# Banded attention by whole and half key tiles in a streaming encoder layer: shared transposes and array halves

## The chip, the core and the metric

The kernel runs on one core of a Trainium2 chip. The metric is the device time of one launch in microseconds (us), the median of several runs. Engines are named as in the profile: PE is TensorE (PEld its weight loads), DVE is VectorE, ACT is ScalarE, POOL is GpSimd, SP is SyncE, which issues all DMAs here. PSUM is where TensorE writes; a bank holds 128 x 512 fp32 numbers.

## The reference

One layer over 2048 new frames (the prompt) and 8 running streams of 16 frames each (the sample), d_model 1024. Cut to what matters here:

```python
# attention: 8 query heads, 2 kv heads of 64; chunk c (64 frames) reads chunks c-2, c-1, c
s = jnp.einsum('bcqgrd,bckgd->bcgrqk', qc, kb) * (SWA_HD ** -0.5)
s = jnp.where(valid, s, NEG_INF)                 # the first chunks have fewer keys
p = sink_softmax(s, sinks)                       # one learned sink per head in the denominator
o = jnp.einsum('bcgrqk,bckgd->bcqgrd', p, vb)
# sample: each stream reads 128 cached keys and its own 16
# retention: 4 heads of 128; one chunk, s is the state of a stream
o = (q k^T * decay) v + (q s) * q_decay
s_new = gamma ** t * s + (k * k_decay)^T v       # the sample has a state for each of 8 streams
# then GroupNorm and gate, output projection, LayerNorm, squared-ReLU MLP (4096), LayerNorm
```

All is fp32.

## The kernel before

The 2176 rows are 17 tiles of 128 (tile 16 is the sample), worked in three groups of 5, 6 and 6 tiles. Each group goes through the stages kv, sq, ret, out and mlp, and a tile's name in the profile carries the group and the stage in which it was made (`sw_1ret`: PSUM tile of kind sw, group 1, stage ret). The big products split each operand into a high and a low part and run as three products of the faster fp32r type (`mm3`); the attention's and retention's own products are plain fp32, and so are the transposes, which are products with the identity.

The order of the program is made when it is built. A planner (`Sched`) keeps an estimated clock for each engine. Each piece of work is a generator that yields the time at which it wants to go on; whenever bulk work is emitted, the planner first lets those generators run whose time has come. Every call (`matmul`, `vtt`, `act`, `dma`) carries a cost, by which the planner's clocks move. So a changed cost, or a changed piece, shifts the order of everything after it on each engine's queue. On the chip each queue runs in order and waits on semaphores.

Tiles come from pools with a fixed number of buffers: `u3` (8, SBUF), `w` (10, weights), `raw` (4), and in PSUM `mm` 2, `rt` 2, `sw` 4 banks.

`swa_task` does the attention of the prompt tiles, one after another, beside the projections. For each of a tile's two chunks it makes scores of 192 keys for 4 heads in 2 pairs (`ps`), row maxima, exponentials with sums (`act`), division by the sum (`vts`), and transposes of the probabilities, padded with zeros to two key tiles of 128; then the product with the values (`pv`). Score products use 64 rows of the array, one kv head in the upper and one in the lower half; value products use 64 columns, one kv head in the left and one in the right half. `swa_sample_task` does the same for the sample, two streams at a time. `ret_task` does retention of one head of one tile; for the sample it works in two halves of 4 streams: it loads the old states (`sold`), masks queries (`qp`) and values (`vm`) by stream, adds four products to `op`, makes four new states in one product of 512 columns (`kvs`), and stores them (`sn`).

Beside this, `first_operands`, `right_operands` and `left_operand` prepare and load split combinations of the MLP's weights, for a scheme that forms seven products in place of eight (a pair of them is counted by `made_d`; `EARLY` is 8). `right_operands` works in group 1's stages in `raw` buffers, and from the MLP on in `w` buffers.

Of the kernel before, what the change touches and what calls it, by code (L numbers as in the profile page):

```python
# [9 lines left out]
F32R = mybir.dt.float32r  # L10
# [163 lines left out]
def tile_layer(ctx: ExitStack, tc: tile.TileContext, A: dict, O: dict):  # L174
# [176 lines left out]
    smask = cst[:, C_SM:C_SM + 8]  # L351
# [162 lines left out]
    def first_operands():  # L514

        for j in range(2):
# [9 lines left out]
            for o, t, args in todo:  # L526
# [8 lines left out]
                yield S.ready(out, eng="ACT")  # L535
# [13 lines left out]
    def right_operands():  # L549
# [8 lines left out]
        def put(j, o, src):  # L558
# [4 lines left out]
            held[0] -= tag == "w"  # L563
            acopy(w[:, 0:512], src)
# [280 lines left out]
    def swa_task(tiles, slot, sq_tasks, qTs, kTall, vall, mixs):  # L845
        gsl = [slice(0, 64), slice(64, 128)]
        for ti, t in enumerate(tiles):
# [6 lines left out]
            w0 = 0 if t > 0 else 1  # L854
            for c in range(2):
                lo = 0 if t > 0 else 128
                lo, hi = (max(lo, 64), 256) if c else (lo, 192)
                yield S.soon(qT, kTall[:, k0:k0 + 2 * P])
                while not (room("sw", 2) and room("u3", 2)):
                    yield S.now + 0.3  # L860
                ps = [take("sw", [P, 2, hi - lo]) for g in range(2)]
                pb = [take("u3", [P, 2, 256]) for g in range(2)]
# [6 lines left out]
                mx, nm, den, es, rec = tiny(4), tiny(4), tiny(4), tiny(4), tiny(4)  # L869
                for g in range(2):  # L870
                    vmax(mx[:, 2 * g:2 * g + 2], ps[g])
                    if c == 0:
                        gzero(pb[g][:, :, 192:256])
                    elif t > 0:
                        gzero(pb[g][:, :, 0:64])
                vstt(nm, mx, -1.0, nsink[:, 0:4], ALU.mult, ALU.min)
                vtt(es, nm, sink[:, 0:4], ALU.add)
                yield S.ready(nm, eng="ACT")
                for g in range(2):
                    for hp in range(2):  # L880
                        i = 2 * g + hp
                        act(pb[g][:, hp, lo:hi], ps[g][:, hp, :], AF.Exp, bias=nm[:, i:i + 1], accum=den[:, i:i + 1])
                drop(*ps)
                act(es, es, AF.Exp)
                yield S.ready(den, es, eng="DVE")
                vtt(den, den, es, ALU.add)
                vrecip(rec, den)
                for g in range(2):
                    for hp in range(2):
                        i = 2 * g + hp  # L890
                        vts(pb[g][:, hp, lo:hi], pb[g][:, hp, lo:hi], rec[:, i:i + 1], None, ALU.mult)
                yield S.soon(*pb)
                pts = []
                for g in range(2):
                    while not (room("sw", 1) and room("u3", 1)):
                        yield S.now + 0.3
                    pt = take("sw", [P, 2, 2, P])
                    for w in range(w0, 2):
                        for hp in range(2):
                            transpose(pt[:, w, hp, :], pb[g][:, hp, 128 * w:128 * w + 128])  # L900
                    drop(pb[g])
                    pts.append(take("u3", [P, 2, 2 * P]))
                    copy(pts[g][:, w0:2, :], pt[:, w0:2].rearrange("p w h r -> p w (h r)"))
                    drop(pt)
                yield S.soon(*pts)
                yield from wait_room("sw")
                pv = take("sw", [P, 256])
                for w in range(w0, 2):
                    for g, gs in enumerate(gsl):
                        matmul(pv[gs, :], vall[:, slot[t] - 1 + w, gs], pts[g][:, w, :], w == w0, w == 1)  # L910
                drop(*pts)
                copy(mixs[ti][:, :, 64 * c:64 * c + 64], pv.rearrange("p (j t) -> p j t", j=4))
                drop(pv)


    def swa_sample_task(ti, si, sq_tasks, qTs, kTall, vall, mix):
# [3 lines left out]
        for hb in range(2):  # L920
# [12 lines left out]
            for pr in range(2):  # L933
# [38 lines left out]
                ov = take("sw", [P, 2, P])  # L972
                for i in range(2):
                    n = 2 * pr + i
                    matmul(ov[:, i, :], cv[:, n, :], pts[:, i, :], True, False)
                    matmul(ov[:, i, :], vn[0:32, n, :], pts[0:32, 2 + i, :], False, True)
                drop(pts)
                for g in range(2):
                    gs = slice(64 * g, 64 * g + 64)
                    for i in range(2):  # L980
                        b = 4 * hb + 2 * pr + i
                        copy(mix[gs, :, 16 * b:16 * b + 16], ov[gs, i, 64 * g:64 * g + 64].rearrange("p (j t) -> p j t", j=4))
# [5 lines left out]
    def ret_task(t, h, ps, rope_t, mix):  # L988
# [32 lines left out]
        if smp:  # L1021
            matmul(op, sm, v, True, False)
            for hb in range(2):
                yield from wait_room("u3", 4)
                sold, qp, vm, sn = [take("u3", sh) for sh in ([P, 4, P], [P, 640], [P, 4, P], [P, 4, P])]
                dma(sold, A["st"][h][:, 4 * hb:4 * hb + 4, :])
                gzero(qp)
                vtt(vm, vd.unsqueeze(1).broadcast_to([P, 4, P]),
# [768 lines left out]
```

## Time and profile before

| | us |
|---|---|
| median of 3 runs | 2352.32 (2351.78 to 2355.8) |
| the profiled execution | 2354.53 |
| its span, first to last instruction | 2352.7 |
| TensorE busy | 2305.9 |
| VectorE busy | 1539.3 |
| ScalarE busy | 888.6 |

The span is what the profile shows of one execution; the execution's own time has 1.8 us more around it. An engine's busy time is the sum of its instructions' times without overlap. The mean granted clock of TensorE was 0.994 of full speed.

### The profile page before, as it was taken

To read this page: it belongs to the slowest core of one execution; us is meant where nothing else is said; L and a number is where in the kernel's file an instruction comes from. 1 tells how busy PE (TensorE), PEld (TensorE's weight loads), DVE (VectorE), ACT (ScalarE), POOL (GpSimd) and SP (SyncE) were. 2 spreads that over 40 slices of the span, in tenths; PEclk is the share of its full clock that TensorE was granted. 3 is DMA by queue.
4 is the path that set the end of the run, shared out by engine and by line. 5 is a ranking of instruction groups with operands and counts; after the bars stand their busy time and mean duration, and the time that the engine had idled before them with its cause. 6 is when DMAs were issued, how large, how long until landed. Compare 5 with 4: busy or idle time off the path is not lost. (4 is left out here: it accounts for less than half of the span.)

```text
span 2352.7 us, 33810 instructions
## 1 busy us (share of the span) xinstructions
PE 2305.9 (98%) x12171; PEld 1997.6 (85%) x12171; DVE 1539.3 (65%) x3444; ACT 888.6 (38%) x2137; POOL 88.5 (4%) x185
## 2 busy tenths in 40 slices
PE   9999999999999999999999999999999999999997
PEld 7778789989987777889999988877788899999986
DVE  5767697777776676687666665845555765555567
ACT  5444744444433443374333322233322742222220
POOL 0000000000000000000000000100100000000000
PEclk9999999999999999999999999999999999999999
DMA  8647646656677546768888887633334477777773
GB/s 300 231 181 281 237 171 241 225 208 230 230 267 259 200 176 249 291 228 328 311 327 329 333 327 288 227 142 105 125 115 171 156 244 253 256 255 256 250 258 118
DMA packets 167479, 551.66 MB, mean 234 GB/s; under 512 B 18704, under 2 KB 25104, under 8 KB 167312
## 3 DMA queue, kind: packets, MB, share of 16 engines
q1 hardware_dynamic: 167312, 549.50, 65.2%
q8 instruction: 97, 1.59, 0.3%
q14 instruction: 70, 0.57, 0.1%
HBM read 391.81 MB, written 157.55 MB: 234 GB/s over the span
## 5 line engine op out<-in xcount | busy, mean ns | idle before, releaser
L260 PE MATMUL sw_1mlp<-xT_1out,w_1mlp 128*128 128x384 f32 x1152 | 209.1, 335 | 0.9 <-DMA w_1mlp<-kept 0.6
L260 PE MATMUL sw_2mlp<-xT_2out,w_2mlp 128*128 128x384 f32 x1152 | 209.0, 335 | 0.3 <-DVE kvln_2mlp L293 0.3
L260 PEld LDWEIGHTS sw_1mlp<-xT_1out,w_1mlp 128*128 128x128 f32 x1152 | 202.0, 188 | 5.2 <-DMA w_1mlp<-kept 1.0
L260 PEld LDWEIGHTS sw_2mlp<-xT_2out,w_2mlp 128*128 128x128 f32 x1152 | 202.1, 188 | 4.2 <-DVE kvln_2mlp L293 0.6
L260 PE MATMUL sw_0mlp<-xT_0out,w_0mlp 128*128 128x320 f32 x1200 | 181.0, 309 | 0.5 <-ACT y_0mlp L277 0.5
L260 PEld LDWEIGHTS sw_0mlp<-xT_0out,w_0mlp 128*128 128x128 f32 x1200 | 178.2, 188 | 3.0 <-ACT y_0mlp L277 0.8
L260 PE MATMUL rt_1mlp<-w_1mlp,u_1mlp 128*128 128x512 f32 x510 | 125.8, 391 | 0.1
L260 PE MATMUL rt_2mlp<-w_2mlp,u_2mlp 128*128 128x512 f32 x510 | 125.5, 391 | 0.0
L260 PE MATMUL mm_1mlp<-w_1mlp,u_1mlp 128*128 128x512 f32 x504 | 124.3, 391 | 0.1
L260 PE MATMUL mm_2mlp<-w_2mlp,u_2mlp 128*128 128x512 f32 x504 | 123.8, 391 | 0.0
L260 PE MATMUL mm_0mlp<-w_0mlp,u_0mlp 128*128 128x512 f32 x480 | 117.0, 390 | 0.0
L260 PE MATMUL rt_0mlp<-w_0mlp,u_0mlp 128*128 128x512 f32 x468 | 113.7, 390 | 0.0
L260 PEld LDWEIGHTS rt_1mlp<-w_1mlp,u_1mlp 128*128 128x128 f32 x510 | 95.3, 188 | 19.5 <-DMA w_1mlp<-keptd 0.6
L260 PEld LDWEIGHTS rt_2mlp<-w_2mlp,u_2mlp 128*128 128x128 f32 x510 | 95.4, 188 | 19.0
L260 PEld LDWEIGHTS mm_1mlp<-w_1mlp,u_1mlp 128*128 128x128 f32 x504 | 94.1, 188 | 19.6 <-DMA w_1mlp<-keptd 0.9
L260 PEld LDWEIGHTS mm_2mlp<-w_2mlp,u_2mlp 128*128 128x128 f32 x504 | 94.3, 188 | 18.8
L260 PEld LDWEIGHTS mm_0mlp<-w_0mlp,u_0mlp 128*128 128x128 f32 x480 | 89.5, 188 | 17.9
L260 PEld LDWEIGHTS rt_0mlp<-w_0mlp,u_0mlp 128*128 128x128 f32 x468 | 87.3, 188 | 17.5
L293 DVE TENSOR_TENSOR w_0mlp<-raw_0mlp,w_0mlp 128x512 fp32r<-128x512 f32 (+1 forms) x69 | 63.4, 920 | 55.7 <-PE sw_0mlp L260 26.8
L260 PE MATMUL mm_1ret<-w_1ret,xT_0mlp 128*128 128x512 f32 x360 | 97.6, 409 | 0.8 <-DMA w_1ret<-halves_ret 0.8
L260 PE MATMUL mm_2ret<-w_2ret,xT_1mlp 128*128 128x512 f32 x324 | 91.1, 410 | 0.0
L277 ACT CAST w_0mlp<-raw_0mlp 128x512 fp32r<-128x512 f32 (+1 forms) x69 | 54.4, 805 | 68.4 <-PE sw_0mlp L260 61.6
(838 smaller groups left out, 4615.5 us busy)
## 6 DMA issues: line engine op xcount, KB each, us to landing
w_1mlp<-kept SPq DMA_DIRECT2D x104, 512.0 KB, 6.1
w_2mlp<-kept SPq DMA_DIRECT2D x104, 512.0 KB, 4.1
kept<-w_0mlp SPq DMA_DIRECT2D x98, 512.0 KB, 2.7
w_1mlp<-keptd SPq DMA_DIRECT2D x98, 512.0 KB, 6.7
w_2mlp<-keptd SPq DMA_DIRECT2D x98, 512.0 KB, 4.1
keptd<-w_1mlp SPq DMA_DIRECT2D x42, 512.0 KB, 6.0
keptd<-raw_1ret SPq DMA_DIRECT2D x35, 512.0 KB, 3.0
raw_0mlp<-in_wdn_dram SPq DMA_DIRECT2D x30, 512.0 KB, 4.7
```

The source lines that it names most:

```text
L260: S.run("PE", lambda: nc.tensor.matmul(out, lhsT, rhs, start=start, stop=stop, skip_group_check=again), [out], [lhsT, rhs], cost)
L277: S.run("ACT", lambda: nc.scalar.copy(out, in_), [out], [in_], 0.06 + 0.83e-3 * size(out))
L293: S.run("DVE", lambda: nc.vector.tensor_tensor(out, a, b, op), [out], [a, b], dcost(out))
```

## The change

- `swa_task`: both chunks of a tile are scored and normalised first, each into 192 of the 384 columns of one buffer per kv head. Chunk 0 reads the whole of the first key tile and the first half of the second; chunk 1 the whole of the second key tile and the second half of the first. The whole tiles are transposed one by one; the two halves stand side by side in the buffer, so one transpose (`ph_`) serves both. The value products run first for the whole key tiles (128 rows, 64 columns of the array), then for the halves (64 rows, 64 columns), the two chunks into two banks. The zero fills go away, and the division is done by two products with a broadcast factor in place of four.
- `swa_sample_task`: the value products are made by kv head, into 64 columns of the array each.
- `ret_task`, sample: both halves at once. The small products go to the left and right columns of the array, the products for the new states use its upper and lower rows; the new states are written over the old ones.
- The planner's costs of fp32 products on half the array are multiplied by 0.55, and the least cost of an fp32 product falls from 0.214 to 0.12.
- `first_operands` and `right_operands` ask for the buffer to be free before ScalarE's copy into it is emitted; `right_operands` goes over to `w` buffers also when half of the output stage of group 1 is done, and the operands of the MLP no longer wait for eight prepared pairs.

```diff
-        cost = max(0.110, n * 0.4167e-3 + 0.0135) if rhs.dtype == F32R else max(0.214, n * 1.67e-3)
+        cost = max(0.110, n * 0.4167e-3 + 0.0135) if rhs.dtype == F32R else max(0.12, n * 1.67e-3)
+        if lhsT.shape[0] == 64 or out.shape[0] == 64:
+            cost *= 0.55
...
-                yield S.ready(out, eng="ACT")
+                yield S.ready(out, h, l, eng="ACT")
...
+            yield S.ready(w, eng="ACT")
             acopy(w[:, 0:512], src)
...
-            if j == EARLY:
+            if tag == "raw" and (j == EARLY or late[0]):
...
-        while gi and len(made_d) < EARLY or (what == "dop" and j not in made_d) or j < 2 and j not in made_u:
+        while (what == "dop" and j not in made_d) or j < 2 and j not in made_u:
...
+            win = [(0, 192, 0), (64, 256, 192)] if t > 0 else [(128, 192, 128), (128, 256, 256)]
+            whole = [0 if t > 0 else None, 1]
+            half = [(1, slice(0, 64)), (0, slice(64, 128)) if t > 0 else None]
+            while not room("u3", 2):
+                yield S.now + 0.3
+            pb = [take("u3", [P, 2, 3 * P]) for g in range(2)]
+            mx, nm, den, es, rec = tiny(8), tiny(8), tiny(8), tiny(8), tiny(8)
+            for c, (lo, hi, at_) in enumerate(win):
+                sl = slice(at_, at_ + hi - lo)
                 yield S.soon(qT, kTall[:, k0:k0 + 2 * P])
+                while not room("sw", 2):
                     yield S.now + 0.3
                 ps = [take("sw", [P, 2, hi - lo]) for g in range(2)]
                 for hp in range(2):
                     for g, gs in enumerate(gsl):
                         matmul(ps[g][:, hp, :], qT[gs, 256 * c + 128 * hp:256 * c + 128 * hp + 128],
                                kTall[gs, k0 + lo:k0 + hi], True, True)
                 if c:
                     drop(qT)
+                cs = slice(4 * c, 4 * c + 4)
                 for g in range(2):
+                    vmax(mx[:, 4 * c + 2 * g:4 * c + 2 * g + 2], ps[g])
+                vstt(nm[:, cs], mx[:, cs], -1.0, nsink[:, 0:4], ALU.mult, ALU.min)
+                vtt(es[:, cs], nm[:, cs], sink[:, 0:4], ALU.add)
+                yield S.ready(nm[:, cs], eng="ACT")
                 for g in range(2):
                     for hp in range(2):
+                        i = 4 * c + 2 * g + hp
+                        act(pb[g][:, hp, sl], ps[g][:, hp, :], AF.Exp, bias=nm[:, i:i + 1],
+                            accum=den[:, i:i + 1])
                 drop(*ps)
+                act(es[:, cs], es[:, cs], AF.Exp)
+                yield S.ready(den[:, cs], es[:, cs], eng="DVE")
+                vtt(den[:, cs], den[:, cs], es[:, cs], ALU.add)
+                vrecip(rec[:, cs], den[:, cs])
                 for g in range(2):
+                    r = rec[:, 4 * c + 2 * g:4 * c + 2 * g + 2].unsqueeze(2).broadcast_to([P, 2, hi - lo])
+                    vtt(pb[g][:, :, sl], pb[g][:, :, sl], r, ALU.mult)
+            yield S.soon(*pb)
+            while not (room("sw", 2) and room("u3", 2)):
+                yield S.now + 0.3
+            ph_, pts = take("sw", [P, 2, 2 * P]), [take("u3", [P, 3, 2 * P]) for g in range(2)]
+            hq = P if t > 0 else 64
+            for hp in range(2):
+                for g in range(2):
+                    transpose(ph_[0:hq, g, P * hp:P * hp + P], pb[g][:, hp, P:P + hq])
+            for g in range(2):
+                while not room("sw"):
+                    yield S.now + 0.3
+                pt = take("sw", [P, 2, 2 * P])
+                for c in range(2):
                     for hp in range(2):
+                        if whole[c] is not None:
+                            transpose(pt[:, c, P * hp:P * hp + P], pb[g][:, hp, 256 * c:256 * c + P])
+                drop(pb[g])
+                c0 = 0 if t > 0 else 1
+                copy(pts[g][:, c0:2, :], pt[:, c0:2, :])
+                copy(pts[g][0:hq, 2, :], ph_[0:hq, g, :])
+                drop(pt)
+            drop(ph_)
+            yield S.soon(*pts)
+            while not room("sw", 2):
+                yield S.now + 0.3
+            pv = [take("sw", [P, 256]) for c in range(2)]
+            for c in range(2):
+                for g, gs in enumerate(gsl):
+                    if whole[c] is not None:
+                        matmul(pv[c][gs, :], vall[:, slot[t] - 1 + c, gs], pts[g][:, c, :], True, not half[c])
+            for c in range(2):
+                for g, gs in enumerate(gsl):
+                    if half[c]:
+                        w, qs = half[c]
+                        matmul(pv[c][gs, :], vall[qs, slot[t] - 1 + w, gs], pts[g][qs, 2, :], whole[c] is None, True)
+            drop(*pts)
+            for c in range(2):
+                copy(mixs[ti][:, :, 64 * c:64 * c + 64], pv[c].rearrange("p (j t) -> p j t", j=4))
+            drop(*pv)
...
-                ov = take("sw", [P, 2, P])
+                ov = take("sw", [P, 2, 64])
                 for i in range(2):
                     n = 2 * pr + i
-                    matmul(ov[:, i, :], cv[:, n, :], pts[:, i, :], True, False)
-                    matmul(ov[:, i, :], vn[0:32, n, :], pts[0:32, 2 + i, :], False, True)
+                    for gs in (slice(0, 64), slice(64, 128)):
+                        matmul(ov[gs, i, :], cv[:, n, gs], pts[:, i, gs], True, False)
+                    for gs in (slice(0, 64), slice(64, 128)):
+                        matmul(ov[gs, i, :], vn[0:32, n, gs], pts[0:32, 2 + i, gs], False, True)
...
+            yield from wait_room("u3", 4)
+            hs = [slice(64 * hb, 64 * hb + 64) for hb in range(2)]
+            sold = [take("u3", [P, 4, P]) for hb in range(2)]
+            qp, vm = take("u3", [P, 2, 320]), take("u3", [P, 4, P])
             for hb in range(2):
+                dma(sold[hb], A["st"][h][:, 4 * hb:4 * hb + 4, :])
+            gzero(qp)
+            vtt(vm, vd.unsqueeze(1).broadcast_to([P, 4, P]), smask.unsqueeze(2).broadcast_to([P, 4, P]), ALU.mult)
+            yield S.ready(qp, eng="DVE")
+            vcopy(qp.rearrange("p h (i x) -> p h i x", x=80)[:, :, :, 0:16],
+                  qk[:, 0, :].rearrange("p (h i x) -> p h i x", h=2, x=16))
+            yield S.soon(qp, vm, *sold)
+            while not room("sw", 2):
+                yield S.now + 0.3
+            kvs = [take("sw", [P, 512]) for hb in range(2)]
+            for i in range(4):
+                for hb in range(2):
+                    matmul(op[hs[hb], :], qp[:, hb, 64 * i:64 * i + 64], sold[hb][:, i, :], False, i == 3)
+            for hb in range(2):
+                matmul(kvs[hb], k[hs[hb], :], vm[hs[hb]].rearrange("p b e -> p (b e)"), True, True)
+            drop(qp, vm)
+            for hb in range(2):
+                so = sold[hb].rearrange("p b e -> p (b e)")
+                vstt(so, so, gamma_pow(h, 16), kvs[hb], ALU.mult, ALU.add)
+            drop(*kvs)
+            yield S.ready(*sold, eng="SP")
+            for hb in range(2):
+                dma(O["ret_s"][h][:, 4 * hb:4 * hb + 4, :], sold[hb])
+            drop(*sold)
...
+            if ui == n // 2 and gi:
+                late[0] = True
```

Of `swa_task` and of the sample part of `ret_task` the lines taken out are those printed above; the diff shows the new ones.

## Rows read from the trace of the kernel before

**Rows 1.** The page's engine totals: busy us of each engine (its share of the span) and its number of instructions.

```profile
PE 2305.9 (98%) x12171; PEld 1997.6 (85%) x12171; DVE 1539.3 (65%) x3444; ACT 888.6 (38%) x2137; POOL 88.5 (4%) x185
```

**Rows 2.** The table by stretches, columns: stretch in us, its length, busy us (and number of instructions) of TensorE, of TensorE's weight loads, of VectorE, ScalarE and GpSimd; granted clock, busy share of the DMA engines, GB/s. The kernel's end.

```profile
2337.00:2352.70 15.70, 1.92 (x9) 1.26 (x7) 11.69 (x21) 0.00 (x0) 1.53 (x2) 0.72 0.27 102
```

**Rows 3.** The table of TensorE's waits: who waited, for whom; us in total, times, longest us.

```profile
PE mm_2kv L260 <- ACT kvln_2kv L277: 5.2, 1, 5.2
PE rt_1ret L264 <- ACT y_1ret L273: 4.5, 3, 2.4
PE rt_0mlp L260 <- ACT xT_0out L277: 4.3, 1, 4.3
PE mm_1kv L260 <- ACT kvln_1kv L277: 3.7, 1, 3.7
PE mm_0ret L260 <- DVE w_0ret L293: 2.0, 3, 1.2
PE rt_0ret L260 <- ACT xT_0ret L277: 1.1, 1, 1.1
PE mm_1ret L260 <- DMA w_1ret<-halves_ret: 0.8, 1, 0.8
```

**Rows 4.** The table by stretches, columns as in rows 2: the attention and retention work of the three groups.

```profile
20.00:208.00 188.00, 184.43 (x1014) 146.20 (x1013) 123.42 (x399) 87.84 (x272) 13.01 (x32) 1.00 0.63 236
735.00:990.00 255.00, 248.45 (x1344) 197.50 (x1343) 165.06 (x522) 107.16 (x324) 18.28 (x45) 0.99 0.59 218
1560.00:1790.00 230.00, 229.85 (x1285) 181.93 (x1284) 116.62 (x436) 76.56 (x276) 20.95 (x53) 1.00 0.32 110
```

**Rows 5.** The timeline of TensorE, a value and a score burst of group 1 between bulk work. Columns: start us, us to the end of the last record, engine, line, operation, out<-in, rows*columns of the array, moving operand, number of records.

```profile
781.11 0.86 PE L260 MATMUL mm_1ret<-w_1kv,xT_0mlp 128*128 128x512 f32 x3
781.90 1.08 PE L260 MATMUL sw_1ret<-u_1ret,kvln_1kv 128*64 128x256 f32 x8
782.91 0.92 PE L260 MATMUL sw_1ret<-kvln_1kv,y_1sq 64*128 64x192 f32 x8
783.76 0.44 PE L264 MATMUL rt_1ret<-cst,xT_1ret 128*128 128x128 f32 x2
```

**Rows 6.** The timeline of TensorE, columns as in rows 5: bulk records and eight transposes of probabilities.

```profile
789.10 1.53 PE L260 MATMUL mm_1ret<-w_1kv,xT_0mlp 128*128 128x512 f32 x6
790.47 1.03 PE L264 MATMUL sw_1ret<-cst,u_1ret 128*128 128x128 f32 x8
791.26 0.94 PE L260 MATMUL mm_1ret<-w_1sq,xT_0mlp 128*128 128x512 f32 x3
792.04 0.57 PE L264 MATMUL rt_1ret<-cst,xT_1ret 128*128 128x128 f32 x3
```

**Rows 7.** The timeline of TensorE, columns as in rows 5: the sample tile's retention in group 2: the four small products (eight records) and the large one, of two halves.

```profile
1605.99 1.05 PE L260 MATMUL rt_2ret<-u_2ret,u_2ret 128*128 128x128 f32 x8
1606.88 1.02 PE L260 MATMUL sw_2ret<-u_2ret,xT_2ret 128*128 128x512 f32 x2
...
1614.09 1.02 PE L260 MATMUL sw_2ret<-u_2ret,xT_2ret 128*128 128x512 f32 x2
1615.04 1.08 PE L260 MATMUL sw_2ret<-u_2ret,kvln_2kv 128*64 128x256 f32 x8
```

**Rows 8.** The timeline of TensorE, columns as in rows 5: scores of the sample tile, of two running streams.

```profile
1705.70 0.71 PE L260 MATMUL sw_2ret<-u_2ret,y_2sq 64*64 64x144 f32 x8
1706.34 0.44 PE L264 MATMUL rt_2ret<-cst,xT_2ret 128*128 128x128 f32 x2
```

**Rows 9.** The timeline of TensorE, columns as in rows 5: the sample tile's attention values of two streams.

```profile
1715.37 1.63 PE L260 MATMUL sw_2ret<-u_2ret,u_2ret 128*128 128x128 f32 x8
1716.93 0.73 PE L260 MATMUL mm_2ret<-w_2ret,xT_1mlp 128*128 128x512 f32 x2
```

**Rows 10.** The timeline of TensorE, columns as in rows 5: scores of the first tile's first chunk, which has 64 keys.

```profile
37.55 0.66 PE L260 MATMUL sw_0sq<-kvln_0kv,y_0sq 64*128 64x64 f32 x8
38.15 0.73 PE L260 MATMUL mm_0sq<-w_0kv,xT__3_328 128*128 128x512 f32 x2
```

**Rows 11.** The groups of instructions by line from 740 to 882 us (attention of group 1), VectorE and ScalarE. Columns: line, engine, operation, out<-in, out<-in (partitions x elements), count | busy us, mean ns of one | idle us before, and for whom.

```profile
L303 DVE TENSOR_SCALAR u_1ret<-u_1ret,tiny_1ret 128x192 f32<-128x192 f32 x32 | 8.3, 321 | 0.3
L293 DVE TENSOR_TENSOR xT_1ret<-mm_1ret,xT_1ret 128x256 f32<-128x256 f32 x20 | 7.5, 415 | 2.8 <-PE mm_1ret L260 2.8
L293 DVE TENSOR_TENSOR raw_1ret<-raw_1ret,raw_1ret 128x512 f32<-128x512 f32 x6 | 4.1, 686 | 0.0
...
L277 ACT COPY u_1ret<-sw_1ret 128x512 f32<-128x512 f32 x15 | 8.1, 584 | 9.2 <-PE sw_1ret L264 9.2
L277 ACT COPY y_1sq<-sw_1ret 128x256 f32<-128x256 f32 x9 | 3.3, 370 | 8.4 <-PE sw_1ret L260 8.4
```

**Rows 12.** The timeline of TensorE and of ScalarE around 838 us; in brackets the idle time before, and for whom. Between the two ScalarE lines stand four exponentials (u_1ret<-sw_1ret).

```profile
841.19 0.44 PE L264 MATMUL rt_1ret<-cst,xT_1ret 128*128 128x128 f32 x2 [2.39 <-ACT y_1ret L273]
...
838.31 0.28 ACT L273 ACTIVATE xT_1ret<-mm_1ret 128x128 f32<-128x128 f32 x1 [4.56 <-DVE xT_1ret L293]
...
840.76 0.63 ACT L273 ACTIVATE y_1ret<-rt_1ret,gnh 128x128 f32<-128x128 f32 x2
```

**Rows 13.** The table by stretches again, columns as in rows 2: the stretch soon after the wait at 838 us.

```profile
842.20:845.50 3.30, 3.30 (x15) 3.01 (x13) 1.08 (x3) 0.91 (x2) 0.00 (x0) 0.50 0.00 0
```

**Rows 14.** The table of ScalarE's waits from 735 to 990 us, columns as in rows 3.

```profile
ACT raw_1ret L277 <- DMA keptd<-raw_1ret: 16.9, 7, 5.5
```

More of the change, by code (lines that the diff above doesn't have):

```diff
@@ L853, in swa_task @@
             k0 = (slot[t] - 1) * P
[L854 to L857, printed above, removed]
+            win = [(0, 192, 0), (64, 256, 192)] if t > 0 else [(128, 192, 128), (128, 256, 256)]
[7 more added lines that the diff above has]
+                sl = slice(at_, at_ + hi - lo)
                 yield S.soon(qT, kTall[:, k0:k0 + 2 * P])
-                while not (room("sw", 2) and room("u3", 2)):
+                while not room("sw", 2):
                     yield S.now + 0.3
                 ps = [take("sw", [P, 2, hi - lo]) for g in range(2)]
-                pb = [take("u3", [P, 2, 256]) for g in range(2)]
                 for hp in range(2):
@@ L892, in swa_task @@
[L892 to L913, printed above, removed]
+                    r = rec[:, 4 * c + 2 * g:4 * c + 2 * g + 2].unsqueeze(2).broadcast_to([P, 2, hi - lo])
@@ L1022, in ret_task @@
             matmul(op, sm, v, True, False)
+            yield from wait_room("u3", 4)
+            hs = [slice(64 * hb, 64 * hb + 64) for hb in range(2)]
+            sold = [take("u3", [P, 4, P]) for hb in range(2)]
+            qp, vm = take("u3", [P, 2, 320]), take("u3", [P, 4, P])
             for hb in range(2):
-                yield from wait_room("u3", 4)
-                sold, qp, vm, sn = [take("u3", sh) for sh in ([P, 4, P], [P, 640], [P, 4, P], [P, 4, P])]
-                dma(sold, A["st"][h][:, 4 * hb:4 * hb + 4, :])
@@ L1027, in ret_task @@
-                gzero(qp)
-                vtt(vm, vd.unsqueeze(1).broadcast_to([P, 4, P]),
-                    smask[:, 4 * hb:4 * hb + 4].unsqueeze(2).broadcast_to([P, 4, P]), ALU.mult)
-                yield S.ready(qp, eng="DVE")
-                vcopy(qp[:, 64 * hb:64 * hb + 576].rearrange("p (b x) -> p b x", x=144)[:, :, 0:16],
-                      qk[:, 0, 64 * hb:64 * hb + 64].rearrange("p (b x) -> p b x", x=16))
-                yield S.soon(qp, vm, sold)
-                yield from wait_room("sw")
@@ L1035, in ret_task @@
-                for i in range(4):
-                    matmul(op, qp[:, P * i:P * i + P], sold[:, i, :], False, hb == 1 and i == 3)
-                kvs = take("sw", [P, 512])
-                matmul(kvs, k, vm.rearrange("p b e -> p (b e)"), True, True)
-                vstt(sn.rearrange("p b e -> p (b e)"), sold.rearrange("p b e -> p (b e)"), gamma_pow(h, 16), kvs,
-                     ALU.mult, ALU.add)
-                drop(kvs, qp, vm)
-                yield S.ready(sn, eng="SP")
-                dma(O["ret_s"][h][:, 4 * hb:4 * hb + 4, :], sn)
@@ L1312, in finish @@
         S.until(lambda: all(t[3] for t in tasks))
-    E, turn, taken, at_pair = None, [0], [], [0]
+    E, turn, taken, at_pair, late = None, [0], [], [0], [False]
     warm = take("y", [P, 512])
@@ L1667, in tile_layer @@
             continue
-        S.until(lambda: len(made_d) >= EARLY and not live["raw"])
+        S.until(lambda: not live["raw"])
         e = [take("raw", [P, 2, 512]) for _ in range(4)] + [take("st", [P, 512])]
```

24 lines of the change are left out of this document (3 added, 21 removed).

## Prediction

> **What bounds the kernel.** I read the page's engine totals first. TensorE is busy for 2305.9 of 2352.7 us and no engine stands near it [rows 1]. The kernel ends with 15.7 us in which TensorE is busy for 1.9 [rows 2]: the last normalisations on VectorE, a tail of 13.8 us that the change doesn't touch. So 2352.7 - 2305.9 - 13.8 = 33 us is left for all of TensorE's waits, and the table of waits shows where the largest sit: at the starts of stages, and, of those in attention, 4.5 us behind a ScalarE activation [rows 3]. Next I cut out the three stretches that hold the attention and retention work: TensorE is idle for 3.6, 6.6 and 0.2 us of 188, 255 and 230, while VectorE is busy for 60% of them and ScalarE for 40% [rows 4]. The work that the change edits lies there, so a microsecond taken out of TensorE's stream there should be a microsecond off the end, unless another engine then makes TensorE wait.
>
> A busy TensorE can hide slack, since its instructions overlap, so all prices below are taken from start to start in the timeline. An fp32 product is two records there: the burst of four products of line 260 on the score tiles is "x8" [rows 5]. A bulk record costs 1.37 / 6 = 0.228 us [rows 6]. A lone 128x128 fp32 record costs 0.89 / 8 = 0.111 us at 128 columns; at 512 columns (1615.04 - 1614.09 - 0.10) / 2 = 0.43 us, the 0.10 being the change of array shape priced next [rows 7]. That is 0.84 ns for a column.
>
> **What sharing the array is worth.** Before an attention burst three bulk records take 0.79 us instead of 0.68: entering another array shape costs 0.10 us [rows 5, 6]. The burst of eight value records (128 rows, 64 columns of the array, 256 moving columns) takes 1.01 us [rows 5]. Alone they would take 8 x 0.215 = 1.72. At two at a time they take 4 x 0.215 = 0.86, and 0.15 is the burst's own cost of filling and draining. The score burst (64 rows, 192 columns) gives nearly the same: 4 x 0.161 + 0.15 = 0.79, measured 0.85 [rows 5]. The sample's scores, in two opposite quarters, take 0.64 = 4 x 0.121 + 0.15 [rows 8]. So left with right halves, upper with lower halves, and opposite quarters all share the array today.
>
> **Transposes.** Eight cost 0.79 us, and the bulk work behind them starts 0.10 late (0.78 for three records), so 0.11 us each [rows 6]. A tile goes from 16 to 12, except the first tile, which has 8 in both versions: 15 x 4 x 0.11 = 6.6 us.
>
> **Value products.** Today a tile has two bursts of 1.01 us. After it, one such burst (whole key tiles, both chunks) and then one of four quarter products of 256 columns. If all four quarters run together, that is 2 x 0.215 + 0.15 = 0.58 us; if only two do, 1.01. The saving is 0.43 or nothing for each of 15 tiles, 6.5 or 0 us. No row shows four at once. I take 6.5, because any two of the four differ in a way that a row shows to be shared: by column half, by row half or by both [rows 5, 8]. The first tile keeps its two short bursts. Today value and score bursts stand back to back [rows 5]; after it the first chunk's scores can follow the quarters and the second chunk's stand alone, so the entries into other shapes stay two a tile. The switch from whole to quarter is in the 0.15.
>
> The Trainium skill says (TensorEngine Tiling (Array Packing), Key Properties) that changing the tiling mode drains TensorE and that the tiles of one mode run independently, four of them at 64x64. It speaks both against the added switch and for the four quarters; the drain is the 0.10 and 0.15 read above, and by the second half of the rule the term is the 6.5 us taken.
>
> **The sample's retention.** For each head and half, four 128-column products cost 0.89 us and one 512-column product 2 x 0.43 = 0.86 [rows 7]; two halves make 3.50. After it, the eight small products run in column halves, 8 steps x 0.111 + 0.15 = 1.04. The two large ones run in row halves, 2 x 0.43 + 0.15 = 1.01. Entering and leaving adds 0.20. That is 2.25, a saving of 1.25 x 4 heads = 5.0 us. If the halves did not share, it would be a loss of 4 x 0.5 = 2.0. Rows 5 show both kinds of sharing, so I take 5.0. VectorE also makes the masked values once instead of twice per head. SP issues the same two loads and two stores a head, the loads together and the stores last; the kernel's own wait for them is one instead of two, and TensorE has bulk work to run meanwhile (0.2 us idle in the third stretch) [rows 4].
>
> **The sample's attention values.** A pair of streams takes 1.56 us for eight records, and 0.10 to leave [rows 9]. After it there are four short bursts of two steps each at 64 columns. A step is between 0.054 us (64 x 0.84 ns) and the 0.11 that 64-column records take with 128-wide weights (0.60 = 4 x 0.11 + 0.15) [rows 10]. At the middle, 0.08, the four bursts cost 4 x 0.31 = 1.24, with entry and exit 1.44. The saving is 0.22 (bounds 0 and 0.43) x 4 pairs = 0.9 us (0 to 1.7).
>
> **Edits at no cost.** Softmax scaling: eight multiplies of 192 columns a tile, 8.3 / 32 = 0.26 us of busy time each, become four tensor-by-tensor products of 384 columns. Those lie between 7.5 / 20 = 0.38 (256 columns) and 0.685 (512), say 0.53 [rows 11]. Both make 2.1 us a tile on VectorE, 60% busy [rows 4]. If the cover were gone it would be at most 4 x 0.685 - 2.1 = 0.6 us a tile. ScalarE's copies of transposed tiles go from four at 0.58 to two at 0.58 and two at 0.37 [rows 11], a gain off the path. The zero fills on GpSimd go away, off the path too.
>
> **The order.** The program is ordered by a planner's costs, and these change: a score product from 0.32 to 0.18 us, a value product from 0.43 to 0.24. Measured, they are 0.85 / 4 = 0.21 and 1.01 / 4 = 0.25 [rows 5]. So the planner's time stops running ahead of the chip by about (0.43 - 0.25) x 8 + (0.32 - 0.21) x 8 = 2.3 us a tile. This bears on one stall: at 838.4 TensorE waits 2.39 us for a bank that ScalarE empties only after four exponentials, which stand behind an activation that arrived 4.56 us late [rows 12]. In the 3.3 us soon after it the granted clock is 0.50, the lower of its levels (1.2 GHz), costing half of 3.3, 1.7 us more [rows 13]. The two new waits for a free buffer, ahead of ScalarE's copies of prepared weights, keep it from standing blocked: it waited 16.9 us in seven times on stores of such buffers [rows 14]. The shorter planned stages also leave the planner less time to prepare weights; what is late then is made in the MLP of group 1, in other buffers, and the operands of that MLP no longer wait for it to be loaded. I cost the new order at 0: it could remove the 4.1 us of that stall and part of the remaining waits, some 8 us in all, or add about as many.
>
> **The sum.** 6.6 + 6.5 + 5.0 + 0.9 = 19.0 us. The profiled execution took 2354.5 us (span 2352.7 and 1.8 around it), 2.2 above the median of 2352.3. 2354.5 - 19.0 = 2335.5 for an execution like it, and 2333 against the median.
>
> **The rivals.**
> - *Quarters share only in pairs* (0.22). The 6.5 us go: 2339.5. For it: no row has four tiles at once. Against it: rows 5 and 8.
> - *The gain returns as waits* (0.09). Shorter bursts make TensorE ask sooner for banks that ScalarE and VectorE empty, and all 19 us come back: about 2352. For it: three of the four waits listed for the retention stages are for these two engines [rows 3]. Against it: they are 40% and 60% busy [rows 4]. The Trainium skill has this as a rule (TensorEngine Tiling (Array Packing), PSUM Bottleneck): tiling speeds TensorE and not the emptying of PSUM; by it the time is the unchanged one.
> - *Slower* (0.06). The stall at 838 becomes regular: both chunks' exponentials now come before any transposed tile, and where they stand in ScalarE's queue ahead of a bank's last reader, each tile pays 2.4 + 1.7 = 4.1 us [rows 12, 13]. It cancels the gain at 19 / 4.1, five tiles, and gives a slower kernel from six; at eight of fifteen, 2333 + 33 = 2366. Against it: it happened in one tile of fifteen.
> - *Stalls go too* (0.05): 19 + 8 us, 2325.
>
> **How the numbers follow.** My forecast, four quarters at once and waits as now, has 0.58: 2333. The range of 2325 to 2346 reaches from the vanished stalls over the paired quarters (2339.5) with 7 us of new waits; the last two rivals on the slow side lie above it. A difference under 0.2%, 4.7 us, can hardly be told from no change in this kernel. Faster: 0.58 + 0.22 + 0.05 = 0.85; same 0.09; slower 0.06.
>
> **What would show it.** In the profile after: 12 transposes a tile at 0.11; a value burst of eight whole records in 1.01 us followed by eight 64x64 records in 0.58 (1.01 would show the pairing rival); the sample's eight small and two large products in about 1.0 us each; TensorE's idle time in the three stretches still near 10 us. A much larger idle time behind ScalarE or VectorE, or new stretches at a granted clock of 0.5, would make the prediction wrong.

## The result and the profile after

The changed kernel takes 2324.94 us (median of 4 runs, 2323.19 to 2326.38) against 2352.99 (2351.78 to 2355.8) for the kernel before beside it: a ratio of 0.9878, interval 0.9865 to 0.9891. It is 28.0 us faster. I had forecast 19 us, and a range that ends at 2325, 0.06 us above the measured median. The profiled execution took 2325.2 us, 29.3 less than that of before; its span is 2323.4.

The engine totals, columns as in [rows 1]:

```profile
PE 2282.5 (98%) x12143; PEld 1980.1 (85%) x12143; DVE 1544.7 (66%) x3401; ACT 870.4 (37%) x2104; POOL 77.1 (3%) x119
```

The three stretches of [rows 4] and the kernel's end, as in [rows 2]. From group 1 on the stages start 2 to 30 us earlier, so the stretches hold slightly different work:

```profile
20.00:208.00 188.00, 186.61 (x1029) 148.32 (x1028) 124.52 (x391) 86.75 (x274) 11.83 (x17) 1.00 0.63 237
735.00:990.00 255.00, 250.33 (x1361) 201.40 (x1358) 173.75 (x513) 106.18 (x322) 15.41 (x24) 1.00 0.60 218
1560.00:1790.00 230.00, 230.00 (x1338) 181.81 (x1337) 125.91 (x435) 72.28 (x262) 17.10 (x34) 1.00 0.38 135
2308.00:2323.40 15.40, 1.25 (x6) 0.71 (x4) 11.03 (x20) 0.00 (x0) 1.53 (x2) 0.71 0.28 103
```

TensorE is idle for 1.4, 4.7 and 0 us (3.6, 6.6 and 0.2 before). The tail is nearly the same: 15.4 - 1.3 = 14.1 us without TensorE's work, 13.8 before. TensorE's waits, as in [rows 3]:

```profile
PE mm_2kv L263 <- ACT kvln_2kv L280: 4.7, 1, 4.7
PE mm_1kv L263 <- ACT kvln_1kv L280: 4.0, 1, 4.0
PE rt_0mlp L263 <- ACT xT_0out L280: 3.9, 1, 3.9
PE rt_1ret L267 <- ACT y_1ret L276: 2.1, 2, 1.7
PE rt_1ret L263 <- DVE state L302: 1.7, 3, 0.6
```

The waits at the starts of stages stay. Of those inside the attention stages, `rt_1ret` behind ScalarE shrinks from 4.5 to 2.1 and `mm_0ret` behind VectorE from 2.0 to 0.5, while `rt_1ret` behind VectorE grows from 0.6 to 1.7. Summed over the whole table, TensorE's waits fall from 32.3 to 26.5 us.

The new products, on TensorE's timeline in order: a tile's value products with the next scores; the sample's retention of one head; the sample's attention values of two streams:

```profile
784.41 1.68 PE L263 MATMUL sw_1ret<-u_1ret,kvln_1kv 128*64 128x256 f32 x16
786.01 0.92 PE L263 MATMUL sw_1ret<-kvln_1kv,y_1sq 64*128 64x192 f32 x8
786.87 0.98 PE L263 MATMUL mm_1ret<-w_1sq,xT_0mlp 128*128 128x512 f32 x3
...
1588.59 1.09 PE L263 MATMUL rt_2ret<-u_2ret,u_2ret 128*64 128x128 f32 x16
1589.62 1.13 PE L263 MATMUL sw_2ret<-u_2ret,xT_2ret 64*128 64x512 f32 x4
1590.67 0.44 PE L267 MATMUL rt_2ret<-cst,xT_2ret 128*128 128x128 f32 x2
...
1690.39 1.12 PE L263 MATMUL sw_2ret<-u_2ret,u_2ret 128*64 128x64 f32 x16
1691.44 0.71 PE L263 MATMUL sw_2ret<-u_2ret,y_2sq 64*64 64x144 f32 x8
```

The view puts the whole and the quarter value records on one row, "x16": 786.01 - 784.41 = 1.60 us from start to start, where two bursts of 1.01 were before [rows 5]. A view that opens between the two kinds gives the quarters a row of their own:

```profile
785.42 0.66 PE L263 MATMUL sw_1ret<-u_1ret,kvln_1kv 64*64 64x256 f32 x8
786.01 0.92 PE L263 MATMUL sw_1ret<-kvln_1kv,y_1sq 64*128 64x192 f32 x8
```

So the whole records take 785.42 - 784.41 = 1.01 us and the quarters 0.59: four quarters do share the array. The sample's small products take 1.03 us, its large ones 1.05, its value products 1.05 for two streams.

**The two traces compared.** Over the whole kernel: 60 transposes fewer (400 are 340 now), 6.6 us at 0.11 each; from start to start, value products 6.4 less, sample retention 4.7 less, sample values 2.0 less. That makes 19.7 of 29.3 us. For the rest I measured *lost time*: for each TensorE record, the time to the next record's start less the median of its shape and type in that execution, summed where that is over 0.3 us. It holds waits and the slow clock behind them. It is read from one profiled execution of each kernel, while the times are medians. It falls from 38.9 to 31.9 us. 19.7 + 7.0 = 26.7; 2.6 us stay unassigned.

### The profile page after: what moved, and what is told of

Same layout as the page of the kernel before. It is cut to its first block, busy times and chain, and to the rows that moved or that the text cites. A ratio compares the mean times of both kernels' runs of the same rounds, so it can differ in the third digit from the quotient of the medians.

```text
span 2323.4 us, 33507 instructions
## 1 busy us (share of the span) xinstructions
PE 2282.5 (98%) x12143; PEld 1980.1 (85%) x12143; DVE 1544.7 (66%) x3401; ACT 870.4 (37%) x2104; POOL 77.1 (3%) x119
## 5 line engine op out<-in xcount | busy, mean ns | idle before, releaser
L263 PEld LDWEIGHTS rt_1mlp<-w_1mlp,u_1mlp 128*128 128x128 f32 x510 | 95.2, 188 | 19.7 <-DMA w_1mlp<-keptd 0.7
L263 PEld LDWEIGHTS mm_0mlp<-w_0mlp,u_0mlp 128*128 128x128 f32 x480 | 89.5, 188 | 17.9
```

## The experiments

The forecast put 0 on the order, and lost time fell by 7 us. The expectations below name theories of where that comes from. Theory 1: the planner's truer costs do it. Theory 2: the edits of the waits do it, by keeping ScalarE's queue open; it is split later into 2a (ScalarE standing blocked) and 2b (the condition on eight prepared pairs). Theory 3: the new shape of the attention does it. Behind all three stands the assumption that the parts simply add. A further rival is luck, that any new order would do as well. I split the change into parts: the attention, the sample (values and retention), the costs, and the waits, these last in two: the *buffer waits* (`S.ready` on the buffer ahead of ScalarE's copy) and the *gate* (the flag `late`, and the operands that no longer wait for eight pairs). "Before" is the median of before in the same job; the lost time is that of the profiled execution.

| run | median us (before) | ratio (interval) | lost time us |
|---|---|---|---|
| before | 2352.99 | | 38.9 |
| the whole change | 2324.94 (2352.99) | 0.9878 (0.9865 to 0.9891) | 31.9 |
| only attention | 2356.87 (2354.39) | 1.0012 (1.0004 to 1.0021) | 53.7 |
| only sample | 2347.43 (2354.39) | 0.9974 (0.9964 to 0.9984) | 39.4 |
| only costs | 2355.34 (2354.39) | 1.0004 (0.9995 to 1.0013) | 41.8 |
| only waits | 2345.99 (2354.39) | 0.9968 (0.9956 to 0.9981) | 31.6 |
| only buffer waits | 2349.76 (2353.57) | 0.9983 (0.9974 to 0.9992) | 36.6 |
| all but attention | 2343.43 (2354.39) | 0.9951 (0.9937 to 0.9965) | 35.3 |
| all but sample | 2334.86 (2354.39) | 0.9917 (0.9904 to 0.9931) | 35.0 |
| all but costs | 2340.55 (2354.39) | 0.9939 (0.9927 to 0.9952) | 40.7 |
| all but waits | 2349.36 (2354.39) | 0.9981 (0.9972 to 0.9990) | 48.8 |
| all but buffer waits | 2340.88 (2356.02) | 0.9936 (0.9924 to 0.9948) | 41.9 |
| all but gate | 2332.21 (2356.02) | 0.9904 (0.9890 to 0.9917) | 39.4 |
| attention and costs | 2360.03 (2353.57) | 1.0026 (1.0018 to 1.0035) | 53.9 |
| attention and waits | 2348.22 (2353.57) | 0.9976 (0.9967 to 0.9985) | 45.5 |
| whole, margin 0.4 | 2325.79 (2356.02) | 0.9873 (0.9858 to 0.9888) | 34.0 |
| whole, measured costs | 2328.55 (2356.02) | 0.9889 (0.9875 to 0.9902) | 33.7 |

### The attention alone

```diff
+            win = [(0, 192, 0), (64, 256, 192)] if t > 0 else [(128, 192, 128), (128, 256, 256)]
...
+                        matmul(pv[c][gs, :], vall[qs, slot[t] - 1 + w, gs], pts[g][qs, 2, :], whole[c] is None, True)
```

> The kernel before with the new attention of the prompt tiles alone; the planner's costs, the buffer waits and the sample's products stay as before. By the profile after, the products of this part give 6.6 us (60 transposes at 0.11) and 6.4 us (value products): 2353 - 13 = 2340. Theory 1, the further 8 us of the change come from the planner's new costs: 2340 here. Theory 2, they come from the new waits for free buffers: 2340 here. Theory 3, they come with the new shape of the attention itself (one chain a tile in place of two): 2332 here.

Measured: 2.5 us slower, which no theory had expected, though its transposes and value products are 13 us shorter here too. Lost time grows by 53.7 - 38.9 = 14.8 us. The two largest of TensorE's waits in this run, both new in size:

```profile
PE mm_0ret L260 <- DVE w_0ret L293: 5.6, 4, 2.7
PE mm_0ret L260 <- DVE xT_0ret L299: 5.3, 1, 5.3
```

In the first, bulk products of group 0 reach weights (`w_0ret`) whose low part VectorE has not made yet. The second can be followed over three engines, on the timelines of ScalarE, VectorE and TensorE (the bracket is the idle time ahead, and who ended it):

```profile
169.62 0.62 ACT L277 CAST st_0ret<-y_0ret 128x512 fp32r<-128x512 f32 x1 [10.62 <-DMA kept<-st_0ret]
...
170.60 0.29 DVE L299 SCALAR_TENSOR_TENSOR xT_0ret<-xT_0ret,mm_0ret 128x128 f32<-128x128 f32 x1 [9.32 <-ACT xT_0ret L277]
...
171.03 1.19 PE L260 MATMUL mm_0ret<-w_0ret,xT__3_328 128*128 128x512 f32 x2 [5.33 <-DVE xT_0ret L299]
```

ScalarE stands 10.62 us at a copy of prepared weights, until the buffer it writes has been stored. Its copies for the queries and keys stand behind that one, VectorE waits for them with a bank still unread, and TensorE for the bank. The table by stretches, in the wait and behind it:

```profile
164.00:169.00 5.00, 1.70 (x8) 1.07 (x6) 0.00 (x0) 0.00 (x0) 0.00 (x0) 0.97 0.81 321
168.70:175.70 7.00, 4.67 (x14) 3.79 (x15) 3.74 (x11) 2.81 (x9) 0.00 (x0) 0.51 0.20 80
```

In the first stretch, which holds the first 3.3 of the 5.3 us, VectorE and ScalarE are busy for 0.00 us while TensorE waits for them. From the wait's last 2.3 us on, the granted clock is 0.51 for 7 us. So for this part by itself the rival "The gain returns as waits" is what happened.

### The sample, the costs and the waits alone

```diff
+                    for gs in (slice(0, 64), slice(64, 128)):
+                        matmul(ov[gs, i, :], cv[:, n, gs], pts[:, i, gs], True, False)
...
+                    matmul(op[hs[hb], :], qp[:, hb, 64 * i:64 * i + 64], sold[hb][:, i, :], False, i == 3)
```

> The kernel before with the sample's new products alone (retention in halves, values by kv head). By the profile after, its products give 4.7 and 2.0 us: 2353 - 6.7 = 2346. All three theories say 2346; a time under 2343 would mean that part of the further 8 us comes from here (loads of the states together, half the masking on VectorE), one over 2349 that this part pays for something in group 2.

```diff
-        cost = max(0.110, n * 0.4167e-3 + 0.0135) if rhs.dtype == F32R else max(0.214, n * 1.67e-3)
+        cost = max(0.110, n * 0.4167e-3 + 0.0135) if rhs.dtype == F32R else max(0.12, n * 1.67e-3)
+        if lhsT.shape[0] == 64 or out.shape[0] == 64:
+            cost *= 0.55
```

> The kernel before with the planner's new costs of fp32 products alone: the same work in another order. Theory 1 (the further 8 us come from the costs): 2345, with the waits of the stages kv to ret in groups 0 and 1 down by some 5 us. Theories 2 and 3: 2353 within 3.

```diff
+                yield S.ready(out, h, l, eng="ACT")
...
+            yield S.ready(w, eng="ACT")
...
+            if tag == "raw" and (j == EARLY or late[0]):
```

> The kernel before with the two waits for free buffers, the early move of the weight preparation to other buffers and the dropped condition on eight prepared pairs alone: no product changes. Theory 2 (the further 8 us come from ScalarE no longer standing blocked): 2345, and ScalarE's 16.9 us of waiting on stores of prepared weights in group 1 mostly gone. Theories 1 and 3: 2353 within 3.

Measured: the sample 7.0 us faster, as its products are 6.7 us shorter. The costs alone give nothing (the interval holds 1), so theory 1 by itself is out. The waits alone, without one product changed, give 8.4 us, as theory 2 expected; lost time falls by 7.3.

### One part left out

Each is the changed kernel without one part of the diffs above.

```diff
-            win = [(0, 192, 0), (64, 256, 192)] if t > 0 else [(128, 192, 128), (128, 256, 256)]
```

> The changed kernel with the old attention of the prompt tiles. Its products cost 13 us more: 2325 + 13 = 2338. Theory 3 (the further 8 us come with the new shape of the attention): 2346. Theories 1 and 2: 2338.

```diff
-                    matmul(op[hs[hb], :], qp[:, hb, 64 * i:64 * i + 64], sold[hb][:, i, :], False, i == 3)
```

> The changed kernel with the old products of the sample. By the products 2325 + 6.7 = 2332, by every theory; more than 2335 would mean that the sample's part carries some of the further 8 us.

```diff
-            cost *= 0.55
```

> The changed kernel with the planner's old costs of fp32 products: the same work, another order. Theory 1: 2333, with the waits in kv to ret up by some 5 us. Theories 2 and 3: 2325 within 3.

```diff
-            yield S.ready(w, eng="ACT")
...
-            if tag == "raw" and (j == EARLY or late[0]):
+            if j == EARLY:
```

> The changed kernel without the two waits for free buffers and with the old conditions on the weight preparation. Theory 2: 2333, and ScalarE waits again some 17 us on stores of prepared weights in group 1. Theories 1 and 3: 2325 within 3.

Measured, by the difference of the ratios to the whole change: without the attention 17 us are lost, without the sample 9, without the costs 14, without the waits 24 (ratio differences times 2353; the intervals leave some 4 us either way). The parts alone sum to -2.5 + 7.0 - 1.0 + 8.4 = 11.9 us, together they give 28.0. So 16 us exist only in combination (by the intervals, some 6 us either way): the parts don't add, and no one of the theories is enough. By adding, at most 8 us were expected to go with the costs or with the waits; 14 and 24 went. The attention, worth nothing alone, is worth 17 us beside the others.

Where it goes without the costs (TensorE's waits, first row of the table):

```profile
PE mm_0ret L260 <- DVE w_0ret L293: 5.4, 5, 2.1
```

It is the wait that the attention alone had; in the whole change it has no row above 0.5 us. VectorE's third product for these weights ends at 116.4 us here, and TensorE starts on them at that moment; in the whole change the third ends at 103.0. Without the waits, the table shows other places:

```profile
PE rt_1mlp L263 <- DMA w_1mlp<-kept: 6.8, 1, 6.8
PE rt_1ret L267 <- ACT y_1ret L276: 4.1, 3, 3.1
PE rt_0ret L267 <- ACT y_0ret L276: 3.2, 1, 3.2
PE sw_1mlp L263 <- DMA w_1mlp<-kept: 2.5, 2, 1.3
```

### The waits taken apart

```diff
-                yield S.ready(out, h, l, eng="ACT")
+                yield S.ready(out, eng="ACT")
...
-            yield S.ready(w, eng="ACT")
```

> The changed kernel without the two waits for free buffers alone; the new conditions on the weight preparation stay. Theory 2a (ScalarE's standing blocked costs most of the 24 us that lie between this kernel without all waits, 2349, and the changed one, 2325): 2340 or more, and ScalarE waits some 40 us on stores again. Theory 2b (the old condition on eight prepared pairs costs most, by late loads at the start of group 1's MLP): 2333 or less, and no wait of TensorE for loads of the MLP's operands.

```diff
-            if tag == "raw" and (j == EARLY or late[0]):
+            if j == EARLY:
...
-        while (what == "dop" and j not in made_d) or j < 2 and j not in made_u:
+        while gi and len(made_d) < EARLY or (what == "dop" and j not in made_d) or j < 2 and j not in made_u:
```

> The changed kernel with the old conditions on the weight preparation alone (eight prepared pairs before any operand of group 1's MLP is loaded); the two buffer waits stay. Theory 2a: 2330 or less. Theory 2b: 2337 or more, with TensorE waiting some 10 us for those loads at the start of group 1's MLP and a stretch of granted clock at 0.5 after it.

The third has the buffer waits as the only change to the kernel before.

```diff
-                yield S.ready(out, eng="ACT")
+                yield S.ready(out, h, l, eng="ACT")
...
+            yield S.ready(w, eng="ACT")
```

> The kernel before with the two waits for free buffers alone. If they account for the whole gain of the four order edits without new products (2346 against 2354): 2346 here, with TensorE's waits in group 1's attention down by some 4 us. If the condition on eight prepared pairs has part in it already where nothing is shorter: 2350.

Measured: the whole change loses some 14 us without the buffer waits, as 2a expected, and 6 without the gate, between what 2a and 2b expected; the buffer waits alone give 3.8 us. Both have a part. What the single edits inside the gate are worth wasn't measured. ScalarE's waits on the stores of buffers that it writes next, without the buffer waits and then in the whole change:

```profile
ACT raw_1ret L280 <- DMA keptd<-raw_1ret: 21.3, 6, 8.5
ACT st_0ret L280 <- DMA kept<-st_0ret: 9.1, 2, 8.5
ACT w_1mlp L280 <- DMA keptd<-w_1mlp: 6.3, 5, 2.2
```

```profile
ACT w_1mlp L280 <- DMA keptd<-w_1mlp: 5.9, 4, 2.7
ACT raw_1ret L280 <- DMA keptd<-raw_1ret: 4.3, 4, 2.0
```

All rows of the kind sum to 52.1 us before (the largest is in [rows 14]), 45.3 here, 12.6 in the whole change. It is the wait that the chain over three engines began with. TensorE's waits in the retention stages of groups 0 and 1 are 13.4 us without the buffer waits and 5.2 with them.

The gate's part is on the DMA queue's own timeline (SPq; columns: start, us from the first to the end of the last, queue, line, operation, out<-in, number). The kernel before, the whole change, and the change without either kind of wait:

```profile
1030.57 0.33 SPq L339 DMA_DIRECT2D keptd<-raw_1out  x1
1030.98 11.36 SPq L339 DMA_DIRECT2D w_1out<-kept  x8
```

```profile
989.65 0.32 SPq L342 DMA_DIRECT2D keptd<-raw_1out  x1
992.18 0.85 SPq L342 DMA_DIRECT2D w_1out<-kept  x2
1024.13 4.22 SPq L342 DMA_DIRECT2D w_1out<-kept  x6
```

```profile
1023.93 16.52 SPq L342 DMA_DIRECT2D keptd<-raw_1out  x3
1040.55 6.37 SPq L342 DMA_DIRECT2D w_1mlp<-kept  x10
```

Before, the eighth pair is stored at 1031, and the MLP of group 1 starts at 1043 with its first loads issued. Without either kind of wait the MLP could start at 1038, 5 us earlier, but the eighth pair is stored at 1040, 9 us later than before, and only then do the loads go out: that is the wait of 6.8 us. The whole change stores seven pairs by 990 and loads from 992. With the gate alone left out, the same wait stands there:

```profile
PE rt_1mlp L263 <- DMA w_1mlp<-kept: 6.5, 1, 6.5
```
 In the run without either kind of wait, the clock is at 0.51 of full from inside the wait on, in the table by stretches:

```profile
1040.00:1050.20 10.20, 4.77 (x18) 4.61 (x19) 5.06 (x12) 6.99 (x16) 0.51 (x1) 0.51 0.91 345
```

At 1.2 GHz in place of 2.4, the 4.77 us in which TensorE worked there did what takes half of that at the full clock: 2.4 us more.

### The attention with one more part

```diff
+            cost *= 0.55
...
+            win = [(0, 192, 0), (64, 256, 192)] if t > 0 else [(128, 192, 128), (128, 256, 256)]
```

> The kernel before with the new attention of the prompt tiles and the planner's new costs, but no buffer waits, the old conditions and the old products of the sample. If the edits simply add: 2358. If true costs are what lets the attention through: 2345, with the 11.6 us of waits in group 0's retention stage under the attention alone back at 5 or less; from the kernel without all waits (2349 with the sample's 7 us) the sum says 2356.

```diff
+            yield S.ready(w, eng="ACT")
...
+            win = [(0, 192, 0), (64, 256, 192)] if t > 0 else [(128, 192, 128), (128, 256, 256)]
```

> The kernel before with the new attention of the prompt tiles, the two buffer waits and the new conditions on the weight preparation, but old planner costs and old products of the sample. If the edits simply add (2357 alone, 8 off for the waits): 2349. If the waits are what lets the attention's 13 us through: 2341 to 2345. Old costs left in the changed kernel cost 15 us, so it should not come under 2340.

Measured: with the costs 6.5 us slower than before, with the waits (buffer waits and gate) 5.4 us faster; with both, which is the run without the sample, 19.5 faster. The pairs come out near the sum of their parts (3.4 slower and 5.9 faster), the three together 14.6 us above it (5.0): the gain needs all three. With the costs alone, `rt_1mlp` waits 6.6 us for its loads, and lost time in that MLP is 14.0 us against 2.1 with both. With the waits alone, `mm_0ret` waits 6.1 us for VectorE's `w_0ret`, and lost time in group 0's retention stage is 10.3 us against 1.7 with both. So each of the two edits takes away a wait that the other leaves. Why old costs make the weights late is argued only: they plan the attention longer than it is, and so may place VectorE's work for the next weights later than TensorE needs it.

### Is it luck?

```diff
-MARGIN = 0.3
+MARGIN = 0.4
```

> The changed kernel with the planner's margin between a result and the TensorE work that reads it at 0.4 instead of 0.3 us: the same work and nearly the same plan, another order. It measures what the order is worth by chance: if the lost waits are owed to the edits, within 4 us of 2325; if the new order was luck, 2330 to 2340.

```diff
-            cost *= 0.55
+            cost *= 0.64 if out.shape[0] == 128 else 0.35 if lhsT.shape[0] == 64 and n == 256 else 0.6
```

> The changed kernel with the planner's factors for half the array set to what the bursts measure (0.64 for 64 rows, 0.60 for 64 columns, 0.35 for the quarter products) in place of 0.55. If a truer cost is what removes waits, 2320 to 2325; if 0.55 was already near enough, 2325 within 4; over 2329 would say that the order's gain doesn't follow the truth of the costs.

`MARGIN` is the time that a piece waits beyond its inputs' planned readiness, so another value reorders every queue. Measured: 0.9873 and 0.9889 against 0.9878 for the whole change, and the three intervals overlap. Two other orders give the same time, so luck is unlikely, as far as two orders can show it. Costs nearer to the measured bursts bring no more either; no version beat the changed kernel beyond the interval.

## Where the prediction was right, and the step that failed

The measured median lies just below the range of 2325 to 2346. The products came as forecast, 19.7 us for 19.0; the step that failed is the 0 for the order.

- **Transposes**: 6.6 us forecast; measured, 60 fewer at the same 0.11 us, which is 6.6.
- **Value products**: 6.5 forecast, 6.4 measured; quarters 0.59 us against 0.58. "Quarters share only in pairs" (1.01) is out. The Trainium skill's rule (TensorEngine Tiling (Array Packing), Key Properties), by which tiles of one mode run independently, agrees: 0.59 us against 1.01 for whole records of as many columns, half the multiplications.
- **The sample's retention**: 5.0 forecast, 4.7 measured; bursts 1.03 and 1.05 against 1.04 and 1.01.
- **The sample's attention values**: 0.9 forecast with bounds 0 and 1.7, measured 2.0, outside. The mechanism was right, the term mis-sized: I took 0.08 us for a step of 64 columns, between two rows. Measured are 1.05 / 4 = 0.26 us a burst, which is 2 x 0.054 + 0.15: the lower end. At that end the forecast was 1.7; the remaining 0.3 or so is an entry of 0.10 us for each of the four pairs, which I charged to the new version alone.
- **Edits at no cost**: held. VectorE's busy time rose by 5 us in total, and no wait on the new softmax products is listed.
- **The order**, costed at 0, is the step that failed. I had the size of what it might remove ("some 8 us in all"), and gave "Stalls go too" 0.05 and 2325; that is what came. Lost time fell by 7.0 us, and the edits of the waits alone, with no product changed, made the kernel 8.4 us faster. TensorE's idle time in the three stretches, expected near 10 us as before, is 6.1. The error is not only the size: I treated the order as one term to be added to the products' 19 us. The runs show that the products' gain depends on it: from the same 13 us of shorter products, the attention makes the kernel 2.5 us slower with the old order's rules and, with costs and waits, the run without the sample is 19.5 us faster.
- **The rival "The gain returns as waits"** had 0.09. It is true of the attention alone, but not by the road that I gave. I argued against it from busy shares of 40% and 60%; what grew were waits for weights not yet prepared (5.6 us), for a bank that two idle engines left unread behind a store (5.3) and, with the costs added, for loads held back until the eighth pair (6.6). A busy share says nothing of an engine that stands blocked. The Trainium skill's rule that emptying PSUM may become the bottleneck (same page, PSUM Bottleneck) fits the second by its place and not by its cause: VectorE and ScalarE did 0.00 us of work in its first 3.3 us.
- **The stall at 838** (TensorE's idle time begins at 838.8, not 838.4): partly removed, 4.5 to 2.1 us behind ScalarE, and no tile repeats it at that length (the longest is 1.7), so "Slower" is out.
- I named the late weights myself ("what is late then is made in the MLP of group 1") and priced them with no row: the rows on the DMA queue of before, a last store at 1031 for an MLP at 1043, showed 12 us of slack. Of the forecast gain 8.7 us lay ahead of that MLP (ten of the fifteen tiles, 0.44 + 0.43 us each), so the gain alone left some of the slack. What the forecast had no term for is the store: without the edits of the waits it came 9 us later, 2 us after the MLP could start. Why it came later wasn't settled.

**What stays open.** Products and lost time together give the measured difference to within 6 us in the runs above, one profiled execution each (the whole change 26.7 of 28.0; all but costs 17.9 of 13.8; all but waits 9.8 of 5.0; attention and costs 2.0 us slower of 6.5). What the remaining few us of those last ones are, spread in gaps of under 0.3 us or in the spread between executions, wasn't settled.

## What to carry to other kernels

A faster piece in a planned order is worth its own time only if what it runs past keeps up: before adding up savings, list for each later stage what must be ready when it starts, with its slack, and compare the slack with the gain and with how much later the new order may make it. Costs of a planner and conditions between its pieces are then part of the change and not an edit at 0. Take a change apart in both directions, each part alone and each part left out; here the parts alone gave 12 us and together 28.

## What the runs showed of the hardware

- Four fp32 products on the four quarters of the array run at once: eight 64x64 records of 256 columns take 0.59 us, eight 128x64 records of 256 columns, which share two at a time, 1.01. Changing from whole to quarter records costs nothing beyond the 0.15 us of a burst (2 x 0.215 + 0.15 = 0.58).
- Records of 64 columns in column halves take 0.26 us a burst of two steps, as if they cost their columns alone: 2 x 0.054 + 0.15.
- A wait costs more than its length. In and behind the 6.8 us wait for loads the granted clock was 0.51 for 10.2 us, and from the last 2.3 us of the 5.3 us wait on it was 0.51 for 7.0.
- An in-order engine that waits for a store's completion holds up unrelated work: ScalarE stood 52.1 us in the kernel before on stores of weight buffers, and with the buffer waits alone (9.1 us left), with not one product changed, the kernel gained 3.8 us.
